# Feed-forward activations turned through memory in place of TensorE transposes, with the down products half a unit later

## The chip, the cores and the metric

One core of a Trainium2 chip runs the whole kernel. The metric is device time in microseconds (us) of one execution; lower is better. Engines are named as in the profile: PE (TensorE matmul), PEld (its weight load), DVE (VectorE), ACT (ScalarE), POOL (GpSimd), SP (SyncE, which here only issues DMAs).

## The reference

One layer on 256 tokens of width 2048 in float32: a mixer (an RWKV-7 half and a gated delta rule half), an output product, and a gated feed-forward block. Only the last part is touched here:

```python
x = x + y @ w_out[l]
h = rms_norm(x, ffn_norm_w[l])
x = x + (jax.nn.silu(h @ ffn_w_gate[l]) * (h @ ffn_w_up[l])) @ ffn_w_down[l]
return rms_norm(x, final_norm_w)
```

with `ffn_w_gate` and `ffn_w_up` of 2048 x 5632 and `ffn_w_down` of 5632 x 2048.

## The kernel before

Every float32 product is made of three products of halves: an operand is split into a high part (rounded to the matmul's own type, `wh`, by ACT, L202) and the rest (`wl`, by DVE, L203), and high x high, low x high and high x low are added up in PSUM. `load_split` (L177) fetches 512 KB of weights into one of three `raw` buffers with a DMA issued by SP (L184) and splits it in two halves of 512 columns into one of two pairs of `wh` and `wl`. All of this has high priority (`hi()`).

The feed-forward block takes the 44 blocks of 128 hidden columns in 11 units of four (`units`, c = 0, 4, ..., 40). For each unit:

- `gate(c1)` and `up(c1, sg)` call `gate_up` (L1049): 8 loads, and for each load 12 products (L1070) of 128 x 512 into two banks, one for each 128 tokens. The stationary operand is the activation x2 (hidden on partitions), the moving one the weights, so the result has tokens on partitions. ACT makes silu of the gate into `sg` (L1081), DVE multiplies the up result in (L1089).
- The down product needs the opposite: hidden columns on partitions, tokens in the free dimension. `turn(c1, sg)` (L1092) makes eight PE transposes of 128 x 128 (L1102) into PSUM banks `psT` and splits them into the tile `h` (high part in columns 0 to 255, rest in 256 to 511 of each of four blocks; L246 and L247).
- `down(c, h, hf)` (L1134), for half hf of the output columns: 4 loads, 12 products (L1147) for each, into four banks `psd` taken in turn from three tags, which DVE then adds to `acc` (L1155). `between` is called after the second load's products.

The order around the change is written out in the loop: gate of the next unit, first down of this unit, up of the next unit, second down of this unit with the next unit's turn in its middle. `beside` is a hook in `gate_up`, used in the first gate to turn x2 for the residual (`turn_x2`). The tiles of an engine are ordered by a list scheduler at build time, from priorities and a simulated timeline; `together` ties some instructions into a sequence on one engine. In unit 9 (c0 = 36) `gate_up` also fetches the down weights of the last unit (`raw_end`, L1062) one after another through one buffer and splits them into places handed out by `wend_slots` (`wend`), for the final products (L1196 to L1198).

The block way through memory that the change uses exists earlier in the kernel: `tri_inverse` stores a tile to DRAM in packets of 128 bytes (`sX`, L360), reads it back (`st`, L363) and turns 32 x 32 blocks on DVE (L369).

Of the kernel before, what the change touches and what calls it, by code (L numbers as in the profile page):

```python
# [49 lines left out]
def trunk_kernel(ctx, tc, xT, vecs, fnw, w_up, a_up, g_up, w_in, w_ab, w_out, w_gu, w_dn, out):  # L50
# [9 lines left out]
    def hi():  # L60
        return tc.high_priority(offset=HI)

    def together(ms, after=(), sync=True):

        kind = mybir.DependencyClass
        for a in after:
            tc.add_manual_dep(ms[0].ins, a.ins.name, mybir.DependencyInfo(kind.Sync, mybir.DependencyReason.DATA),
                              reason="together")
        for a, b in zip(ms, ms[1:]):
            tc.add_manual_dep(b.ins, a.ins.name, mybir.DependencyInfo(kind.NoSync, mybir.DependencyReason.DATA),  # L70
                              reason="together")

    def mps(name, tag="mr"):
        return pm.tile([P, 512], F32, tag=tag, name=name)
# [73 lines left out]
    class Side:  # L148
# [4 lines left out]
        def step(self):  # L153
            if self.cond is not None:
                if not self.cond():
                    return False
                self.cond = None
            try:
                self.cond = next(self.gen)
            except StopIteration:  # L160
                self.done = True
                side.remove(self)
            return True
# [8 lines left out]
            assert any([g.step() for g in list(side)])  # L172


    first = []

    def load_split(src, by_k=False, whole=False):  # L177

        with hi():
            if first:  # L180
                raw = first.pop(0)
            else:
                raw = wp.tile([P, 1024], F32, tag="raw", name="raw", bufs=RAW)
                SY.dma_start(out=raw.rearrange("p (c f) -> p c f", c=4) if by_k else raw, in_=src)  # L184
            wh = wp.tile([P, 1024], F32R, tag="wh", name="wh", bufs=WH)
            wl = wp.tile([P, 1024], F32R, tag="wl", name="wl", bufs=WL)
            both = [(wh[:, h * 512:h * 512 + 512], wl[:, h * 512:h * 512 + 512]) for h in range(2)]
            if whole:
                split(wh, wl, raw)
                return both  # L190
            it = iter(both)
            return halves_of(raw, lambda: next(it), by_k)
# [856 lines left out]
    def gate_up(c0, m, tag="pb", beside=None):  # L1049

        banks = [pm.tile([P, 512], F32, tag=tag, name="psq") for _ in range(2)]
        b = c0 + 2 * m - NFB + 8
        ends = [(x % 4, x // 4) for x in (b, b + 1, b + 4, b + 5)] if 0 <= b < 4 else []
        for q in range(2):
            for kk in range(4):
                if ends and kk % 2:
                    wend[ends[2 * q + kk // 2]] = halves_of(raw, own)
                elif ends:
                    raw = rp.tile([P, 1024], F32, tag="i1", name="raw_end")
                    i_, hf = ends[2 * q + kk // 2]  # L1060
                    with hi():
                        SY.dma_start(out=raw, in_=w_dn[NFB - 4 + i_, hf])  # L1062
                parts = load_split(w_gu[c0:c0 + 4, m, q, :, kk * 256:kk * 256 + 256].rearrange("c p f -> p c f"), True)
                for kx in range(2):
                    k = 8 * q + 2 * kk + kx
                    t, ri = x2k[k]
                    wh, wl = parts[kx]
                    for o, w in ((0, wh), (T, wh), (0, wl)):
                        for tb in range(2):
                            last = PE.matmul(banks[tb], t[:, ri, o + tb * P:o + tb * P + P], w,  # L1070
                                             start=(k == 0 and o == 0 and w is wh), stop=(k == KB - 1 and w is wl))
                if beside and kk % 2:
                    beside(2 * q + kk // 2, last)
        return banks

    def gate(c0, beside=None):
        banks = gate_up(c0, 0, beside=beside)
        sg = [fp.tile([P, 512], F32, tag="tg", name="sg", bufs=2) for _ in range(2)]
        with hi():
            for tb in range(2):  # L1080
                S.activation(sg[tb], banks[tb], AF.Silu, scale=rstd2[:, tb:tb + 1])  # L1081
        last_gate[0] = sg[1]
        return sg

    def up(c0, sg, tag="pb"):
        banks = gate_up(c0, 1, tag)
        with hi():
            for tb in range(2):
                V.scalar_tensor_tensor(sg[tb], banks[tb], rstd2[:, tb:tb + 1], sg[tb], ALU.mult, ALU.mult)  # L1089
        return sg  # L1090

    def turn(c0, sg, before=()):  # L1092

        h = act.tile([P, 4, 2 * T], F32R, tag="act", name=f"h{c0}")
        ps, ms = [], []
        for b in range(2):
            ps.append(mps("psT", ("mr", "mc", "mg")[nbank[0] % 3]))
            nbank[0] += 1
            for i in range(2):
                for tb in range(2):  # L1100
                    o = i * T + tb * P
                    ms.append(PE.transpose(ps[b][:, o:o + P], sg[tb][:, (2 * b + i) * P:(2 * b + i) * P + P], ident))  # L1102
        together([*before, *ms])
        for b in range(2):
            with hi():
                p3, hs = ps[b].rearrange("p (i t) -> p i t", i=2), slice(2 * b, 2 * b + 2)
                split(h[:, hs, 0:T], h[:, hs, T:], p3)
        return h

    nbank = [0]  # L1110

    def wend_slots():

        one = ["lw", "SB", "sq2", "bk", "i3"] + ["kt", "rt"] * 2 + ["vt"] * 4
        bufs = {"kt": 2, "rt": 2, "vt": 4}

        def places():
            x2w = rp.tile([P, 8, 512], F32R, tag="AT1", name="wend")
            for i in range(8):
                yield x2w[:, i, :]  # L1120
            w = act.tile([P, 4, 2 * T], F32R, tag="act", name="wend")
            for i in range(4):
                yield w[:, i, :]
            w = rp.tile([P, 2, 512], F32R, tag="Yt", name="wend")
            yield w[:, 0, :]
            yield w[:, 1, :]
            for t in one:
                yield rp.tile([P, 512], F32R, tag=t, name="wend", bufs=bufs.get(t, 1))
            for i in range(6):
                yield fp.tile([P, 512], F32R, tag=("wend", "sq2")[i // 4], name="wend", bufs=(4, 2)[i // 4])  # L1130
        g = places()
        return lambda: (next(g), next(g))

    def down(c0, h, hf, between=None):  # L1134
        n = 4
        banks = []
        for b in range(4):
            banks.append(mps("psd", ("mr", "mc", "mg")[nbank[0] % 3]))
            nbank[0] += 1
        for i in range(n):  # L1140
            parts = load_split(w_dn[c0 + i, hf])
            for tb in range(2):
                hh = h[:, i, tb * P:tb * P + P]
                hl = h[:, i, T + tb * P:T + tb * P + P]
                for st, w in ((hh, 0), (hh, 1), (hl, 0)):
                    for cg in range(2):
                        m = PE.matmul(banks[tb * 2 + cg], st, parts[cg][w],  # L1147
                                      start=(i == 0 and w == 0 and st is hh), stop=(i == n - 1 and st is hl))
            if between and i == 1:
                between(m)  # L1150
        for tb in range(2):
            for cg in range(2):
                cs = slice(hf * 1024 + cg * 512, hf * 1024 + cg * 512 + 512)
                with hi():
                    V.tensor_tensor(acc[:, tb, cs], acc[:, tb, cs], banks[tb * 2 + cg], ALU.add)  # L1155
# [3 lines left out]

    def turn_x2(i, before):  # L1160

        tb, ps = i // 2, [mps("ps_xn", t) for t in ("mr", "mc")]
        q0 = i % 2 * 2
        ms = [PE.transpose(ps[q][:, k * P:k * P + P], x2[:, 4 * (q0 + q) + k, tb * P:tb * P + P], ident)
              for q in range(2) for k in range(4)]
        together([before] + ms)
        for q in range(2):
            S.copy(acc[:, tb, (q0 + q) * 512:(q0 + q) * 512 + 512], ps[q])

    sg = gate(units[0], turn_x2)  # L1170
    h = turn(units[0], up(units[0], sg, "mg"))

    for c, c1 in zip(units, units[1:]):
        sg = gate(c1)
        down(c, h, 0)
        up(c1, sg)
        ahead = []
        down(c, h, 1, lambda m: ahead.append(turn(c1, sg, [m])))
        h = ahead[0]


    n = 4
# [110 lines left out]
```

## Time and profile before

| | |
|---|---|
| median of 3 runs | 1256.82 us (1255.65 to 1258.12) |
| profiled execution | 1255.44 us, of which the span of the profile is 1253.7 |
| granted PE clock | 0.995 |
| feed-forward block (first product of L1070 at 510.03 us) | about 740 us of the span |
| PE in the window of one unit, 591.65 to 657.84 | busy 66.19 of 66.19 us |
| DMA engines in the same window | 67% busy, 189 GB/s |

A row of the profile like `PE psT L1102` names the engine, the tile written and the line. In the chain of waits the first number is the start in us from the start of the span, the second the length, and `x8` the number of instructions. In rows of groups the two numbers behind the bar are busy time in us and the mean ns of one, and behind the next bar stands the idle time ahead of them and who ended it. Rows of waits give total us, times, and the longest. A row of a window gives the window, its length, each engine's busy time with its instructions (PE, PEld, DVE, ACT, POOL), and then the granted clock, the DMA engines' busy share and GB/s. DMA rows of a queue give packets, MB and the share of 16 engines' time.

### The profile page before, as it was taken

The page shows a single profiled execution, that of the slowest core. Times are in us where ns is not written, and L with a number is a line of the kernel's source. Part 1 is how long each engine was busy: PE and PEld are TensorE (multiplying, and loading weights), DVE is VectorE, ACT ScalarE, POOL GpSimd, SP SyncE. Part 2 cuts the span into 40 slices and gives each one's busy share as a digit, 9 for nine tenths or more (in the row PEclk, how much of TensorE's full clock was granted, in tenths as well). Part 3 has the DMA queues.
Part 4 walks back from the last instruction along what each step waited for, and adds up shares of the span by engine and source line. Part 5 has one row for each costly group of instructions (what it writes and reads, how often), then busy time and mean ns, then how long its engine had stood idle before and what let it go on. Part 6 is the DMA issues. An engine that isn't in the chain of part 4 may idle for free.

```text
span 1253.7 us, 21133 instructions
## 1 busy us (share of the span) xinstructions
PE 1234.8 (98%) x8134; PEld 1087.0 (87%) x8134; DVE 834.3 (67%) x1635; ACT 651.3 (52%) x1199; POOL 17.8 (1%) x63
## 2 busy tenths in 40 slices
PE   8999999999999999999999999999999999999997
PEld 8999999999999989888888888888888888878886
DVE  7987887977966877565555555555656565665554
ACT  7575665667546456554444444444444444454443
POOL 3000000000000000000000000000000000000000
PEclk9999999999999999999999999999999999999999
DMA  7455665575573445676666666666676666676641
GB/s 248 153 169 179 169 170 149 169 186 139 196 213 118 145 159 186 172 205 194 190 190 197 188 193 192 194 190 196 187 198 182 189 190 195 203 236 193 193 151 67
DMA packets 175702, 226.68 MB, mean 181 GB/s; under 512 B 52273, under 2 KB 144561, under 8 KB 175345
## 3 DMA queue, kind: packets, MB, share of 16 engines
q1 hardware_dynamic: 170896, 221.54, 60.4%
q10 hardware_dynamic: 4560, 2.74, 0.8%
q8 instruction: 64, 1.05, 0.4%
q0 software_dynamic: 144, 1.05, 0.2%
q14 instruction: 38, 0.30, 0.1%
HBM read 218.75 MB, written 4.46 MB: 178 GB/s over the span
## 4 chain that ended last, share of the span: by engine, by line
PE 88%; DVE 5%; DMA 3%; issue 1%; ACT 1%; SPq 0%; ACTq 0%; DVEq 0%
PE psq L1070 37%; PE psd L1147 17%; PE psb L220 16%; PE psb L223 8%; DVE wl L247 2%; PE psT L1102 1%; DMA sX_r<-X_r 1%; DMA raw_end<-in_w_dn 1%; DMA st_r<-sX_r 1%; PE ps_A L485 1%; PE psd L1198 1%; PE psd L1196 1%; PE psd L1197 1%; DMA A_g<-sG 0%; PE psSg L923 0%
## 5 line engine op out<-in xcount | busy, mean ns | idle before, releaser
L203 DVE TENSOR_TENSOR wl<-raw,wh 128x512 fp32r<-128x512 f32 x524 | 340.7, 692 | 273.5 <-ACT wh L202 271.8
L202 ACT ACTIVATE wh<-raw 128x512 fp32r<-128x512 f32 x524 | 302.5, 626 | 363.9 <-PE psq L1070 192.4
L1070 PE MATMUL psq<-wh,x2s 128*128 128x512 f32 x1408 | 377.4, 390 | 0.8 <-ACT wh L202 0.8
L1070 PEld LDWEIGHTS psq<-wh,x2s 128*128 128x128 f32 x1408 | 263.7, 188 | 56.2 <-ACT wh L202 1.7
L1070 PE MATMUL psq<-wl,x2s 128*128 128x512 f32 x704 | 217.2, 389 | 0.0
L220 PE MATMUL psb<-xs,wh 128*128 128x256 f32 x816 | 206.4, 287 | 2.4 <-ACT wh L202 1.7
L223 PE MATMUL psb<-xs,wh 128*128 128x256 f32 x816 | 206.0, 286 | 0.0
L1147 PE MATMUL psd<-wh,h 128*128 128x512 f32 x640 | 203.2, 391 | 1.0 <-ACT wh L202 1.0
L246 ACT ACTIVATE wh<-raw 128x1024 fp32r<-128x1024 f32 x128 | 135.4, 1058 | 87.4 <-PE psb L223 67.8
L247 DVE TENSOR_TENSOR wl<-raw,wh 128x1024 fp32r<-128x1024 f32 x128 | 156.1, 1220 | 11.1 <-ACT wh L246 10.9
L220 PEld LDWEIGHTS psb<-xs,wh 128*128 128x128 f32 x816 | 156.8, 192 | 4.4 <-ACT wh L202 2.4
L223 PEld LDWEIGHTS psb<-xs,wh 128*128 128x128 f32 x816 | 156.8, 192 | 1.2 <-issue 0.7
L1070 PEld LDWEIGHTS psq<-wl,x2s 128*128 128x128 f32 x704 | 132.0, 188 | 27.6
L1147 PEld LDWEIGHTS psd<-wh,h 128*128 128x128 f32 x640 | 119.2, 188 | 25.8 <-ACT wh L202 1.7
L220 PE MATMUL psb<-xs,wl 128*128 128x256 f32 x816 | 127.1, 287 | 0.9 <-DVE wl L247 0.7
L1147 PE MATMUL psd<-wl,h 128*128 128x512 f32 x320 | 124.6, 389 | 0.0
L220 PEld LDWEIGHTS psb<-xs,wl 128*128 128x128 f32 x816 | 109.8, 192 | 2.8 <-DVE wl L247 1.1
L1147 PEld LDWEIGHTS psd<-wl,h 128*128 128x128 f32 x320 | 60.1, 188 | 12.7
L223 PE MATMUL psb<-ys,wh 128*128 128x256 f32 x256 | 64.6, 288 | 2.5 <-DVE ys L247 2.5
L220 PE MATMUL psb<-ys,wh 128*128 128x256 f32 x256 | 64.8, 289 | 0.2 <-ACT ys L246 0.2
L223 PEld LDWEIGHTS psb<-ys,wh 128*128 128x128 f32 x256 | 50.1, 196 | 2.8 <-DVE ys L247 2.7
L1155 DVE TENSOR_TENSOR acc<-acc,psd 128x512 f32<-128x512 f32 x80 | 49.5, 682 | 1.8 <-PE psd L1147 1.8
(315 smaller groups left out, 1026.8 us busy)
## 6 DMA issues: line engine op xcount, KB each, us to landing
raw<-in_w_gu SPq DMA_DIRECT2D x176, 512.0 KB, 4.9
raw<-in_w_in SPq DMA_DIRECT2D x99, 512.0 KB, 3.5
raw<-in_w_dn SPq DMA_DIRECT2D x80, 512.0 KB, 4.3
raw<-in_w_out SPq DMA_DIRECT2D x32, 512.0 KB, 3.5
raw_end<-in_w_dn SPq DMA_DIRECT2D x8, 512.0 KB, 4.2
xraw<-in_xT SPq DMA_DIRECT2D x8, 256.0 KB, 5.8
x<-in_xT SPq DMA_DIRECT2D x1, 2048.0 KB, 9.7
raw<-in_w_ab SPq DMA_DIRECT2D x2, 512.0 KB, 4.9
```

The costliest lines, as they stand in the source:

```text
L202: S.activation(oh, src, AF.Copy)
L203: V.tensor_tensor(ol, src, oh, ALU.subtract)
L220: PE.matmul(ps[:, 0:T], w, rt[:, ri, 0:T], start=(first and k == 0 and not low), stop=(last and k == 7 and low == 1))
L223: PE.matmul(ps[:, 0:T], w, rt[:, ri, T:], start=False, stop=False)
L246: S.activation(hi_ap, src, AF.Copy)
L247: V.tensor_tensor(lo_ap, src, hi_ap, ALU.subtract)
L485: PE.matmul(psA[h][:, ch, :], bk[hr, ch].rearrange("p a t -> p (a t)"), ar[hr, p, ch].rearrange("p a t -> p (a t)"), start=True, stop=True)
L1070: last = PE.matmul(banks[tb], t[:, ri, o + tb * P:o + tb * P + P], w, start=(k == 0 and o == 0 and w is wh), stop=(k == KB - 1 and w is wl))
L1102: ms.append(PE.transpose(ps[b][:, o:o + P], sg[tb][:, (2 * b + i) * P:(2 * b + i) * P + P], ident))
L1147: m = PE.matmul(banks[tb * 2 + cg], st, parts[cg][w], start=(i == 0 and w == 0 and st is hh), stop=(i == n - 1 and st is hl))
L1155: V.tensor_tensor(acc[:, tb, cs], acc[:, tb, cs], banks[tb * 2 + cg], ALU.add)
L1196: PE.matmul(ps, hh, wh, start=(i == 0), stop=False)
```

## The change

Units 0 to 9 are no longer turned by PE. `turn_far(c0, sg)` makes two VectorE block transposes (`V.transpose`, 32 x 32 blocks, on 128 x 512 each) into tiles `tn0` and `tn1` (tags i2 and i3), which puts the tokens of each block of 32 into the free dimension but leaves the blocks where they were. Eight DMAs of 64 KB store `tn` in a DRAM tile `sH` in runs of 128 bytes, and four DMAs of 128 KB read it back, in runs of 1 KB, into the second half of the tile `h`, with the hidden columns on partitions. One split over all four blocks then makes the high and the low part. All twelve DMAs are issued by SP, each group tied behind the last weight load (`loads[-1]`). They are placed by the hook `step`, which is now called after every load's products in both gate and up of the next unit: stores at steps 2 to 5 (in the gate), reads at steps 8 to 11 and the split at step 14 (in the up).

The downs of a unit come half a unit later to give this the time: gate of the next unit, second down of the unit before last (`late`), up of the next unit, first down of this unit. The last unit is turned by PE as before, in the last second down. The i3 slot is taken from the places of the last unit's weights.

```diff
-                SY.dma_start(out=raw.rearrange("p (c f) -> p c f", c=4) if by_k else raw, in_=src)
+                loads.append(SY.dma_start(out=raw.rearrange("p (c f) -> p c f", c=4) if by_k else raw, in_=src))
...
-                if beside and kk % 2:
-                    beside(2 * q + kk // 2, last)
+                if beside:
+                    beside(4 * q + kk, last)
...
-    def up(c0, sg, tag="pb"):
-        banks = gate_up(c0, 1, tag)
+    def up(c0, sg, tag="pb", beside=None):
+        banks = gate_up(c0, 1, tag, beside)
...
+    def turn_far(c0, sg):
+
+        tn = []
+        for tb in range(2):
+            tn.append(rp.tile([P, 512], F32, tag=("i2", "i3")[tb], name=f"tn{tb}"))
+            with hi():
+                V.transpose(tn[tb], sg[tb])
+        h = act.tile([P, 4, 2 * T], F32R, tag="act", name=f"h{c0}")
+        raw = h[:, :, T:].bitcast(F32)
+
+        sH = dr.tile([32, 16, 8, 32], F32, name=f"sH{c0}")
+        rows = sH.rearrange("r (i q) b c -> q r i (b c)", q=4)
+
+        def step(n, last):
+            with hi():
+                if 2 <= n < 6:
+                    tb, a0 = n // 2 - 1, n % 2 * 2
+                    ds = [SY.dma_start(out=sH[:, :, 4 * tb + a, :],
+                                       in_=tn[tb][32 * a:32 * a + 32].rearrange("r (j c) -> r j c", c=32))
+                          for a in (a0, a0 + 1)]
+                elif 8 <= n < 12:
+                    ds = [SY.dma_start(out=raw[32 * q:32 * q + 32], in_=rows[q]) for q in (n - 8,)]
+                else:
+                    ds = []
+                if ds:
+                    together([loads[-1]] + ds)
+                if n == 14:
+                    split(h[:, :, 0:T], h[:, :, T:], raw)
+        return h, step
...
-        one = ["lw", "SB", "sq2", "bk", "i3"] + ["kt", "rt"] * 2 + ["vt"] * 4
+        one = ["lw", "SB", "sq2", "bk"] + ["kt", "rt"] * 2 + ["vt"] * 4
...
     def turn_x2(i, before):
 
+        if i % 2 == 0:
+            return
+        i //= 2
...
     sg = gate(units[0], turn_x2)
-    h = turn(units[0], up(units[0], sg, "mg"))
-
+    h, step = turn_far(units[0], up(units[0], sg, "mg"))
+
+    late = None
     for c, c1 in zip(units, units[1:]):
-        sg = gate(c1)
+        sg = gate(c1, step)
+        if late:
+            down(*late, 1)
+        up(c1, sg, "pb" if late else "mg", lambda n, last: step(8 + n, last))
         down(c, h, 0)
-        up(c1, sg)
-        ahead = []
-        down(c, h, 1, lambda m: ahead.append(turn(c1, sg, [m])))
-        h = ahead[0]
+        late = c, h
+        if c1 != units[-1]:
+            h, step = turn_far(c1, sg)
+    ahead = []
+    down(*late, 1, lambda m: ahead.append(turn(units[-1], sg, [m])))
+    h = ahead[0]
```

More of the change, by code (lines that the diff above doesn't have):

```diff
@@ L172, in drain @@
             assert any([g.step() for g in list(side)])
-    first = []
+    first, loads = [], []
     def load_split(src, by_k=False, whole=False):
```

## The prediction

> **What bounds the kernel.** I read the page first, then the chain of waits in one feed-forward unit, then who waits for whom on PE, ACT and SP, then the DMA queue in short windows.
>
> ```profile
> span 1253.7 us, 21133 instructions
> PE 1234.8 (98%) x8134; PEld 1087.0 (87%) x8134; DVE 834.3 (67%) x1635; ACT 651.3 (52%) x1199; POOL 17.8 (1%) x63
> ...
> L246 ACT ACTIVATE wh<-raw 128x1024 fp32r<-128x1024 f32 x128 | 135.4, 1058 | 87.4 <-PE psb L223 67.8
> L247 DVE TENSOR_TENSOR wl<-raw,wh 128x1024 fp32r<-128x1024 f32 x128 | 156.1, 1220 | 11.1 <-ACT wh L246 10.9
> ```
> ```profile
> 591.65 21.76 PE psq L1070 x96
> 613.41 5.44 PE psd L1147 x24
> 618.86 0.87 PE psT L1102 x8
> 619.73 5.47 PE psd L1147 x24
> 625.20 21.76 PE psq L1070 x96
> 646.96 10.88 PE psd L1147 x48
> 657.84 21.76 PE psq L1070 x96
> ```
>
> The second fence is the chain of waits over one unit (start, length, what): an up, the second down with the turn in its middle, a gate, the first down, the next up. The chain never leaves PE. From 591.65 to 657.84 a unit lasts 66.19 us and holds 288 products: 21.76/96 = 0.2267 us each, 65.28 in all. The rest, 66.19 - 65.28 = 0.91 us, is the turn (0.87) and the products beside it (5.47 against 5.44).
>
> ```profile
> PE psd L1147 <- ACT wh L202: 1.0, 1, 1.0
> PE psq L1070 <- ACT wh L202: 0.8, 2, 0.5
> ```
> ```profile
> ACT wh L202 <- PE psq L1070: 192.4, 128, 2.1
> ACT wh L202 <- PE psd L1147: 111.0, 74, 2.0
> ACT wh L202 <- DMA raw<-in_w_gu: 32.5, 18, 2.8
> ...
> ACT wend L202 <- DMA raw_end<-in_w_dn: 12.6, 6, 3.3
> ```
>
> These are PE's waits and ACT's waits in this stage (us in total, times, longest). PE waits 1.8 us in it. ACT, which makes the high halves of the weights, mostly waits for PE to give back a buffer (303 us), much less for a weight load (32.5). So PE is the bound, and what leaves PE's queue leaves the time, as long as weights come no later than this:
>
> ```profile
> 671.02 1.16 ACT L202 ACTIVATE wh<-raw 128x512 fp32r<-128x512 f32 x2 [1.56 <-PE psq L1070]
> ...
> 671.88 1.29 DVE L203 TENSOR_TENSOR wl<-raw,wh 128x512 fp32r<-128x512 f32 x2 [1.62 <-ACT wh L202]
> ...
> 674.00 1.07 PE L1070 MATMUL psq<-wh,x2s 128*128 128x512 f32 x4
> ...
> 674.90 0.61 PE L1070 MATMUL psq<-wl,x2s 128*128 128x512 f32 x2
> ...
> 679.41 1.41 DVE L1089 SCALAR_TENSOR_TENSOR sg<-psq,rstd,sg 128x512 f32<-128x512 f32 x2 [0.99 <-PE psq L1070]
> ...
> 690.58 2.48 DVE L1155 TENSOR_TENSOR acc<-acc,psd 128x512 f32<-128x512 f32 x4
> ```
>
> In this timeline the block that PE starts at 674.00 is split at 671.02 (ACT, first half done by 671.60) and 671.88 (DVE, first half done by 672.53, needed at 674.90). A split may thus start 2.4 us late before PE stands. The idle time in brackets (1.56 on ACT) is in every 2.72 us step.
>
> **The change, part by part.**
>
> *Taken off PE.* Units 0 to 9 lose their eight transposes; unit 10 keeps them. 10 x 0.91 = 9.1 us, all on the path. The other products are the same, in another order; the turning of x2 (turn_x2) happens at the same four places, since every second call of eight now returns at once. Between gate and up lies now the second down of the unit before; the accumulators alternate as before, so I cost the reordering at nothing. What covers it is the evacuation beside the next products (2.48 us of DVE above, with PE not waiting). Only at the end do two downs follow each other, and the second needs two of the first's banks 6 products (1.36 us) in: 0 to 1 us, once; I take 0.3.
>
> *Added on DVE and ACT.*
>
> ```profile
> L369 DVE STREAM_TRANSPOSE tn_r<-st_r x2: 446/446/446, 185.8 to 271.1; 128x256 f32<-128x256 f32 x2
> ...
> L246 ACT ACTIVATE h<-psT x22: 579/584/599, 562.2 to 1219.0; 128x512 fp32r<-128x512 f32 x22
> L247 DVE TENSOR_TENSOR h<-psT,h x22: 682/684/692, 562.8 to 1219.9; 128x512 fp32r<-128x512 f32 x22
> ```
> ```profile
> 591.65:657.84 66.19, 66.19 (x298) 54.89 (x297) 38.17 (x61) 29.88 (x52) 0.00 (x0) 1.00 0.67 189
> ```
>
> Two block transposes of 512 columns, 2 x 2 x 0.446 = 1.8 us a unit on DVE. The splits of h change from two of 0.584 and 0.684 to one of 1.06 (ACT) and 1.22 (DVE). By the windows row DVE is busy 38.17 of 66.19 us and would be 39.8 of 65.3. A transpose of 0.9 or a split of 1.2 fits an idle gap of some 1.4, and the 2.48 of L1155 passes without a wait of PE. Cost taken: nothing; bounds 0 to 0.3 us a unit.
>
> *Added on SP and the DMA engines.* Per unit eight stores of 64 KB (512 packets of 128 bytes each), two behind each of four gate loads, and four loads of 128 KB (128 packets of 1 KB each) behind four up loads.
>
> ```profile
> DMA packets 1811, 0.26 MB, mean 171 GB/s; under 512 B 1804, under 2 KB 1804, under 8 KB 1811
> ...
> q1 hardware_dynamic: 1811, 0.26, 103.3%
> ```
> ```profile
> DMA packets 9480, 12.50 MB, mean 189 GB/s; under 512 B 381, under 2 KB 8453, under 8 KB 9477
> ...
> q1 hardware_dynamic: 9477, 12.46, 67.2%
> ```
> ```profile
> L360 SPq DMA_DIRECT2D sX_r<-X_r x4: 551/660/827, 177.8 to 261.3; - x4
> ```
> ```profile
> SPq L184 <- DVE wl L203: 504.5, 228, 3.7
> ```
>
> The first fence is the window 180.0 to 181.5, when the triangular inverse stores 128-byte packets in DRAM: 1811 packets with all engines busy, so 1.5 x 16 / 1811 = 13.3 ns a packet, 0.85 us for the 1024 of one step. The second is the unit above: 24 weight loads take 67.2% of 66.19 us, 1.85 us each. A step with stores needs 1.85 + 0.85 = 2.70 of its 2.72 us: the queue is full for four steps but falls behind by nothing. A read step adds 128 packets at no more than the unit's mean of 44.5 x 16 / 9477 = 75 ns, 0.6 us, which fits. On SP two stores are issued in 2 x 0.66 = 1.3 us, inside the 504.5/228 = 2.2 us that it waits before each load for DVE to free a raw buffer; behind them stand only later loads. Cost taken: nothing.
>
> The DMA page of the Trainium skill (DMA: Bandwidth & Descriptors, Specifications) speaks against this: below 512 bytes the DMA does a read-modify-write. If that doubled my 13.3 ns the gain would be gone (worked out under the rivals), but those 13.3 ns are themselves stores of 128 bytes to DRAM, so the row already holds it, and the row decides.
>
> *New waits.* The stores wait on SP for the transposes. SP runs ahead:
>
> ```profile
> 670.29 8.49 SPq L184 DMA_DIRECT2D raw<-in_w_dn  x4
> ...
> 679.44 1.07 PE L1147 MATMUL psd<-wh,h 128*128 128x512 f32 x4
> ```
>
> a load is issued 9.2 us before its products, so the third gate load goes out 3.7 us before the gate, 7.2 after the end of the up (a down of 10.88 lies between). The transposes are done 1.4 + 1.8 = 3.2 us after the up. Unit 0 has no down there: if SP's order holds the first store at that place, SP stands some 6 us and PE at most 6 - 2.4 = 3.6, once. I take 0.3, since the order of an engine's queue is laid out ahead of time with work that can run put first: in the chain's rows on unit 0
>
> ```profile
> 536.27 25.46 PE psq L1070 x112
> 561.74 0.87 PE psT L1102 x8
> ```
> ```profile
> raw<-in_w_gu SPq DMA_DIRECT2D x176, 512.0 KB, 4.9
> ...
> sX_r<-X_r SPq DMA_DIRECT2D x4, 128.0 KB, 4.6
> ```
>
> the up's 96 products are followed by 16 of the next gate, and only then by the turn, which the program has first. The reads come at least three loads (8 us) behind the stores, against 4.6 us from issue to landing of the sX_r stores on the page. The split of h then stands in ACT's order, ahead of the next weight split, until the last read has landed. Its cover is ACT's 1.56 us gap and the 2.4 above: a wait w costs PE w + 1.06 - 1.56 - 2.4 us, nothing up to 2.9. The nearest row is ACT's wait for raw_end, 12.6/6 = 2.1 us, longest 3.3. I take 0; bounds 0 to 0.4 a unit.
>
> ```profile
> 1088.50:1112.73 24.23, 22.39 (x97) 17.46 (x96) 15.23 (x25) 12.83 (x24) 0.00 (x0) 1.00 0.81 261
> ```
>
> *The last weights.* In the gate of unit 9, raw_end loads come on top and the gate lasts 24.23 us instead of 21.76: 2.5 us already lost to waits like these. Here the stores come on top again, and the i3 slot is gone from the list of places: bounds from -2.5 (the loads move to another place and the loss goes) to +4 x 0.85 = +3.4; I take +0.5.
>
> **Sum.** The profiled execution took 1255.44 us (span 1253.7). 1255.44 - 9.1 + 0.3 + 0.3 + 0.5 = 1247.4. The median of the runs shown is 1256.82, 1.4 above the profiled one, so 1248.8 is my time, 0.64% faster.
>
> **Rivals.**
>
> *The h split eats part of it.* ACT waits for the read in its order longer than the cover. At 3.3 us, the longest raw_end wait, it costs 0.4 us a unit: 1253. With the bounds of DVE (0.3) and unit 9 too, 1255. For: DMA landings that ACT's order didn't foresee stand in the rows. Against: six such waits in a gate at 81% DMA cost 2.5 us together.
>
> *Slower: the same wait at full length.* From w = 3.8 us on, the loss (0.91 a unit) outweighs the turn. If ACT stood a whole landing of a gate load (4.9 us on the page), 4.9 + 1.06 - 1.56 - 2.4 = 2.0 a unit, 1256.8 + 10 x (2.0 - 0.9) = 1268. The rows' 3.3 stays short of the point.
>
> *Slower or even: dear packets.* Stores at a stride of 1 KB, beside weights, might cost more than those of the inverse. With p ns a packet four steps fall behind by 4 x (1.85 + 0.064 p - 2.72); less the 2.4 of cover this reaches 0.91 at p = 26.5, twice the row: then no change. At 40 ns it is 6.8 - 2.4 - 0.9 = 3.4 a unit, 1290.
>
> *It does nothing:* the weights can't come 1.4% faster, and the time goes from the turn to waits for wh, 1255 to 1257. Against it: ACT waits for PE, not for loads, in 303 us, and DMA has a third of its time left.
>
> **Chances.** My forecast 0.62 (own range 1245.5 to 1251.5); the h split eating part 0.16 (three quarters of it still below 1254.3); nothing 0.08; the long wait 0.08; dear packets 0.06, a third of it at no change. About 0.2% (2.5 us) is what a measurement here tells from no change. Faster: 0.62 + 0.12 = 0.74. Same: 0.04 + 0.08 + 0.02 = 0.14. Slower: 0.12. The range 1245.5 to 1257.5 leaves out the slower cases and a few percent below.
>
> **What the profile after would show.** Right: psT with 8 transposes instead of 88; units of 65.3 us in the chain; two STREAM_TRANSPOSE of about 0.89 us a unit; DMA share of a unit near 0.75; ACT's wait for h below 2.9 us; PE's waits in this stage still a few us. Wrong: PE waiting for wh or wl once in each unit, near the gate's third to sixth load (packets) or behind the split of h (long wait). The store step is wrong if its windows show the DMA engines full and gate loads landing 3 us later than 4.9.

## The result, and the profile after

The changed kernel takes 1266.26 us in the median of 8 runs (1259.45 to 1270.2), the one before 1257.14 of 8 (1255.25 to 1259.74): 0.7% slower, ratio 1.0068 with a 95% interval of 1.0043 to 1.0092. The forecast was 1248.8, and 1257.5 at most.

The page of the changed kernel (span, engines, chain, landing of DMAs):

```profile
span 1266.7 us, 21161 instructions
...
PE 1234.3 (97%) x8054; PEld 1077.5 (85%) x8054; DVE 844.7 (67%) x1645; ACT 649.0 (51%) x1189; POOL 17.8 (1%) x63
...
PE 73%; DMA 12%; DVE 9%; ACT 3%; issue 2%; SPq 1%; ACTq 0%; DVEq 0%
...
raw<-in_w_gu SPq DMA_DIRECT2D x176, 512.0 KB, 5.6
...
sH<-tn SPq DMA_DIRECT2D x80, 64.0 KB, 5.2
h<-sH SPq DMA_DIRECT2D x40, 128.0 KB, 6.2
```

The 80 transposes are gone, and yet PE is busy as long as before (1234.8) in a span 13 us longer. The chain now holds 12% of DMA and 9% of DVE (3 and 5 before). Gate and up weights land 5.6 us after issue, not 4.9. Who waited for whom from 505 us on, PE first, then ACT:

```profile
PE psq L1070 <- ACT wh L202: 11.1, 10, 4.6
```
```profile
ACT wh L202 <- DMA raw<-in_w_gu: 126.7, 63, 4.6
...
ACT wh L202 <- PE psq L1070: 90.9, 71, 3.2
ACT h L246 <- DMA h<-sH: 25.0, 10, 4.8
```

ACT stands 25.0 us for the reads of h, once for each of the ten units turned in this way, and 126.7 us for gate and up loads, which was 32.5. The chain through one unit shows how a wait for h leads to a long wait for a load (most of the 126.7 us stay when no wait for h is left, and cost nothing, as late_split shows below):

```profile
712.83 8.17 PE psd L1177 x36
721.03 0.64 ACT wh L202
721.69 1.30 DVE wl L203 x2
723.01 0.37 SPq L184
723.38 0.05 issue
723.43 6.62 DMA h<-sH
730.07 1.07 ACT h L246
731.16 0.07 DVE h L247
...
732.31 1.30 DVE wl L203 x2
733.62 6.77 DMA raw<-in_w_gu
...
740.50 0.64 ACT wh L202
...
741.18 5.78 PE psq L1070 x24
746.96 10.88 PE psd L1177 x48
```

The last read is issued at 723.43 and lands 6.6 us later. Only then does ACT split h, and behind it in ACT's and DVE's order stand the next weight splits. So a raw buffer comes free late (733.62), the load that it was wanted for lands at 740.4, and now PE stands. From 712.83 to 746.96 a down and an up took 34.13 us for 144 x 0.2267 = 32.64: 1.49 lost, more than the 0.91 of a turn. ACT's timeline in the same stretch has both waits, each in the brackets:

```profile
726.89 1.15 ACT L202 ACTIVATE wh<-raw 128x512 fp32r<-128x512 f32 x2 [1.99 <-DMA raw<-in_w_gu]
730.07 1.06 ACT L246 ACTIVATE h<-h 128x1024 fp32r<-128x1024 f32 x1 [2.03 <-DMA h<-sH]
731.04 2.18 ACT L202 ACTIVATE wh<-raw 128x512 fp32r<-128x512 f32 x4
734.73 1.15 ACT L202 ACTIVATE wh<-raw 128x512 fp32r<-128x512 f32 x2 [1.52 <-PE psq L1070]
740.50 1.15 ACT L202 ACTIVATE wh<-raw 128x512 fp32r<-128x512 f32 x2 [4.61 <-DMA raw<-in_w_gu]
```

ACT waits 2.03 us for h, catches up, and 5 us later waits 4.61 for a weight load.

The dearest place is unit 0 to 1, where no down lies between up, gate and up (timeline of PE, then windows):

```profile
579.36 1.21 PE L1070 MATMUL psq<-wh,x2s 128*128 128x512 f32 x4 [1.66 <-ACT wh L202]
...
595.15 2.08 PE L1070 MATMUL psq<-wh,x2s 128*128 128x512 f32 x4 [4.57 <-ACT wh L202]
```
```profile
579.36:590.00 10.64, 10.64 (x47) 8.78 (x48) 5.16 (x8) 5.08 (x9) 0.00 (x0) 1.00 0.82 190
595.15:605.00 9.85, 9.85 (x31) 7.86 (x32) 5.41 (x9) 3.81 (x7) 0.00 (x0) 0.69 0.54 133
605.00:614.61 9.61, 9.61 (x44) 7.97 (x43) 4.34 (x8) 3.88 (x7) 0.00 (x0) 1.00 0.64 195
```

PE stands (has no work) 1.66 and 4.57 us, and in the 9.85 us after the long stand its granted clock is 0.69.

The losses by place, here and in the runs below, worked out from the starts of the groups of products in each trace, less 0.2267 us a product and 0.11 a transpose. The first gate's own 4.5 us (the sum of squares and turn_x2) are taken off. The raw_end loads belong to unit 9, but the order laid out at build time may place them earlier (in most of these kernels two of the eight stand beside unit 0): in the kernel before the loss is at the gate of unit 9, in the changed kernel and several others at the gate or up of unit 8. The column takes units 8 and 9 together.

| kernel | unit 0 to 1 | raw_end (units 8 and 9) | other units |
|---|---|---|---|
| before | 0 | 2.9 | 0 |
| changed | 10.5 | 5.3 | 6.6 |
| no_way | 0 | 4.4 | 0 |
| stores_only | 1.8 | 5.8 | 0 |
| reads_only | 10.3 | 4.5 | 4.5 |
| late_split | 2.9 | 4.9 | 0 |
| order_only | 0.6 | 2.8 | 0 |
| late_unit0 | 0 | 6.6 | 0 |
| late_ends | 1.3 | 1.1 | 0 |
| late_ends_5 (the same kernel) | 2.5 | 4.0 | 0 |
| late_unit0_ends | 0 | 2.1 | 0 |
| late_unit0_ends_2 (the same kernel) | 0 | 0.3 | 0 |
| before_ends | 0 | 0 | 0 |

Each row is one profiled execution. The two rows of late_ends differ by 1.2 and 2.9 us, so a difference of that size between single rows is no measured cost; and the row of no_way is from an execution of 1249.3 us, 3.4 below its median.

The changed kernel loses 22.4 us where the one before loses 2.9, and saves 9.1: 10.4 slower in this stage. The two profiled executions differ by 13.0 us, the medians by 9.1. The other 2.5 us between the two spans lie before the stage, in code that both share: the first product of L1070 starts between 509.9 and 513.1 us in the twelve different kernels profiled here (509.9 in the one before, 512.3 in the changed one, 512.7 in before_ends, which turns as before).

### The profile page after: what moved, and what is told of

Read it like the earlier page. It is cut to its first block, busy times and chain, and to the rows that moved or that the text cites. A ratio compares the mean times of both kernels' runs of the same rounds, so it can differ in the third digit from the quotient of the medians.

```text
span 1266.7 us, 21161 instructions
## 1 busy us (share of the span) xinstructions
PE 1234.3 (97%) x8054; PEld 1077.5 (85%) x8054; DVE 844.7 (67%) x1645; ACT 649.0 (51%) x1189; POOL 17.8 (1%) x63
## 4 chain that ended last, share of the span: by engine, by line
PE 73%; DMA 12%; DVE 9%; ACT 3%; issue 2%; SPq 1%; ACTq 0%; DVEq 0%
PE psq L1070 29%; PE psd L1177 15%; PE psb L220 14%; PE psb L223 7%; DMA h<-sH 3%; DMA raw<-in_w_gu 2%; DVE wl L247 2%; DMA raw_end<-in_w_dn 2%; DVE wl L203 1%; DMA raw<-in_w_in 1%; ACT wh L202 1%; DMA sX_r<-X_r 1%; PE ps_A L485 1%; DVE wend L203 1%; PE psd L1237 1%
## 5 line engine op out<-in xcount | busy, mean ns | idle before, releaser
L202 ACT ACTIVATE wh<-raw 128x512 fp32r<-128x512 f32 x524 | 301.1, 623 | 350.0 <-DMA raw<-in_w_gu 126.7
L1070 PE MATMUL psq<-wh,x2s 128*128 128x512 f32 x1408 | 381.4, 393 | 11.3 <-ACT wh L202 11.1
L1070 PEld LDWEIGHTS psq<-wh,x2s 128*128 128x128 f32 x1408 | 264.2, 189 | 71.5 <-ACT wh L202 16.8
L1070 PE MATMUL psq<-wl,x2s 128*128 128x512 f32 x704 | 219.2, 392 | 1.3 <-DVE wl L203 0.7
L1177 PE MATMUL psd<-wh,h 128*128 128x512 f32 x640 | 200.6, 390 | 0.0
L247 DVE TENSOR_TENSOR wl<-raw,wh 128x1024 fp32r<-128x1024 f32 x128 | 156.1, 1220 | 10.3 <-ACT wh L246 10.0
L1070 PEld LDWEIGHTS psq<-wl,x2s 128*128 128x128 f32 x704 | 131.8, 189 | 32.7 <-DVE wl L203 5.2
```

Of the source, the lines that this page charges most:

```text
L202: S.activation(oh, src, AF.Copy)
L247: V.tensor_tensor(lo_ap, src, hi_ap, ALU.subtract)
L1177: m = PE.matmul(banks[tb * 2 + cg], st, parts[cg][w], start=(i == 0 and w == 0 and st is hh), stop=(i == n - 1 and st is hl))
```

## The experiments

Theory 1: ACT's split of h stands in its order until late reads land, and what it holds up comes back as late weight loads. Theory 2: the 128-byte stores fill the DMA queue. Theory 3: the new order, or DVE, costs the time.

**no_way** drops both branches with DMAs in `step` and splits from the block transposes:

```diff
-                    split(h[:, :, 0:T], h[:, :, T:], raw)
+                    for tb in range(2):
+                        o = tb * P
+                        split(h[:, :, o:o + P], h[:, :, T + o:T + o + P], tn[tb].rearrange("p (i t) -> p i t", i=4))
```

> Leaves out all twelve DMAs of each unit; h is split straight from the block transposes (so it holds the wrong tokens and hidden columns), at the same step. Theory 1 (ACT's split of h stands in its order until the reads land, and what it holds up comes back as late weight loads) and theory 2 (the 128-byte stores fill the DMA queue and make the gate loads late) both expect the removed transposes to show: 1248 to 1251 us against 1257 before. Theory 3 (the new order of downs or the DVE transposes cost the time themselves): 1257 or more.

1252.69 us (1247.63 to 1254.08), ratio to before 0.9947 (0.9924 to 0.9969). The median is 1.7 us above the range expected, but theory 3 is out: in the table this kernel loses nothing outside the raw_end column. The saving of the transposes is real; the way through memory takes it.

**stores_only** has the same split and keeps the stores.

> Leaves out the reads; the stores stay, h is split straight from the block transposes (wrong values). Theory 1: nearly all of the loss is gone, 1248 to 1253 us. Theory 2: 1258 us or more, with PE waiting for weights in the gates.

1252.75 us (1251.95 to 1254.01), ratio 0.9962 (0.9947 to 0.9977). The median is that of no_way (1252.69), which has no stores. In the single profiles the eighty stores of 128-byte packets lose 1.8 us in unit 0, 1.4 more at raw_end, which is inside the spread of that column, and nothing in the other units. Theory 2 falls as the main cause.

**reads_only** makes the stores in unit 0 alone:

```diff
+    same = []
...
-        sH = dr.tile([32, 16, 8, 32], F32, name=f"sH{c0}")
+        if c0 == 0:
+            same.append(dr.tile([32, 16, 8, 32], F32, name="sH"))
+        sH = same[0]
...
-                if 2 <= n < 6:
+                if c0 == 0 and 2 <= n < 6:
```

> Leaves out the stores of all units but unit 0; every unit reads unit 0's tile (wrong values). Unit 0 keeps both stores and reads and so its 10.6 us. Theory 1: 1262 to 1266 us, ACT's wait for h stays at 20 to 25 us in all. Theory 2: 1254 to 1259 us, and the gate loads land in 4.9 us again.

1266.27 us (1263.16 to 1269.31), ratio 1.0069 (1.0048 to 1.009): as slow as the changed kernel, as theory 1 had it (0.3 above its range). Gate and up loads land after 5.2 us on its page. ACT's waits in it (from 510 to 1230 us):

```profile
ACT wh L202 <- DMA raw<-in_w_gu: 89.9, 39, 4.5
ACT h L246 <- DMA h<-sH: 22.9, 10, 4.3
```

The wait for h is nearly whole (22.9 of 25.0), with no stores behind unit 0. The other units lose 4.5 us in its profile against 6.6 with stores; whether stores add to the reads there, one profile of each doesn't tell.

**late_split** leaves all twelve DMAs and their places, and ties only ACT's part of the split behind a later weight split:

```diff
-            S.activation(oh, src, AF.Copy)
+            highs.append(S.activation(oh, src, AF.Copy))
...
                 if n == 14:
-                    split(h[:, :, 0:T], h[:, :, T:], raw)
+                    high = S.activation(h[:, :, 0:T], raw, AF.Copy)
+                    V.tensor_tensor(h[:, :, T:], raw, h[:, :, 0:T], ALU.subtract)
+                    together([highs[-1], high])
```

> Computes the whole; ACT's part of the h split is tied behind the weight split of the seventh up load (step 14), some 7 us after the last read lands. Theory 1: the waits of ACT for h go (from 25 us to under 2) and with them 6 to 9 us: 1257 to 1260 us, the loss of unit 0 to 1 stays. Theory 2: no change, 1264 to 1268 us.

1254.58 us (1253.3 to 1256.04), ratio to before 0.9977 (0.9966 to 0.9989): 12 us faster than the changed kernel by the medians, more than expected, since 7.6 of unit 0's 10.5 go as well. The loss of the other units is zero. In the answer on the tile h (changed kernel, then late_split), under "its engine sat idle before it":

```profile
  DMA h<-sH: 25.0, 10
```
```profile
  ACT h L1137: 1.6, 9
```

Nothing waits for a read any more (1.6 us is DVE waiting for ACT), and the reads land as late as before, 6.1 us in the median: the place of the split in ACT's order cost the time, not the amount of data. ACT's waits for gate and up loads (510 to 1230 us) are hardly fewer than the 126.7 us of the changed kernel:

```profile
ACT wh L202 <- DMA raw<-in_w_gu: 108.9, 64, 4.1
```

The loss is gone all the same, outside the first two columns of the table. So these waits as such don't cost PE anything; what cost it, by the chain above, were those that a held-up split made too long for the buffers to cover. A unit in its chain is bare products, 65.28 us:

```profile
705.36 10.88 PE psd L1179 x48
716.24 21.76 PE psq L1070 x96
738.00 10.88 PE psd L1179 x48
748.88 21.76 PE psq L1070 x96
```

**order_only** turns every unit by PE, in the new order:

```diff
-        up(c1, sg, "pb" if late else "mg", lambda n, last: step(8 + n, last))
-        down(c, h, 0)
+        up(c1, sg, "pb" if late else "mg")
+        ahead = []
+        down(c, h, 0, (lambda m: ahead.append(turn(c1, sg, [m]))) if c1 != units[-1] else None)
```

> Computes the whole; the downs in the new order, but every unit turned by PE in the middle of its predecessor's first down; no block transposes, no way through memory. If the new order itself costs nothing (theory 1): within 2 us of before, 1255 to 1259 us. If the order costs: 1260 us or more.

1258.5 us (1256.16 to 1260.83), ratio 1.0008 (0.9996 to 1.0019). The order costs nothing that shows: 1.0 us by this ratio, with an interval from -0.5 to 2.4.

**early_reads** issues the reads at steps 6 to 9 in place of 8 to 11.

> Computes the whole; the changed kernel with the four reads two steps earlier (behind gate loads 7 and 8 and up loads 1 and 2 in place of up loads 1 to 4); the split is not tied. Theory 1a (ACT's place for the split follows the landing that the build-time order assumes, wherever the reads stand): the split moves ahead with them, ACT still waits 2 us or so a unit, 1262 to 1268 us. Theory 1b (the reads are merely too late for a fixed place): the waits go, 1254 to 1257 us.

1314.2 us (1309.7 to 1316.51), ratio 1.0444 (1.0415 to 1.0473). Both expectations missed by 50 us. SP's waits from 580 to 1260 us, and ACT's for h from 505 us on:

```profile
SPq L1131 <- DMA sH<-tn: 21.5, 19, 3.4
```
```profile
ACT h L246 <- DMA h<-sH: 42.4, 9, 5.8
```

Now the first reads follow the last stores by one step and must wait on SP until these have landed (5.2 us on its page). SP stands up to 3.4 us, and the weight loads behind it stand too. The split moved ahead with the reads, as theory 1a has it, but with two changes at once this run doesn't tell 1a from 1b. It shows that one step between the last store and the first read is too little for SP's queue; distances between that and the changed kernel's weren't run.

**late_unit0** is late_split with

```diff
-    h, step = turn_far(units[0], up(units[0], sg, "mg"))
+    h, step = turn(units[0], up(units[0], sg, "mg")), lambda n, last: None
```

> Computes the whole; the tied split of the run late_split, and unit 0 turned by PE as before. Unit 0 has no down between its up and the next gate, so its stores stand close behind the transposes; late_split still loses 2.9 us there. If the way through memory causes that: 1252 to 1254 us (2.9 gained, 0.9 paid for the turn). If it is the raw_end loads beside it: 1255 us, no gain.

1252.31 us (1250.96 to 1252.83), ratio 0.9958 (0.9941 to 0.9975). Unit 0's loss is gone, as expected if the way through memory made it.

**late_ends** is late_split with raw_end loads spread and their splits tied:

```diff
-        b = c0 + 2 * m - NFB + 8
-        ends = [(x % 4, x // 4) for x in (b, b + 1, b + 4, b + 5)] if 0 <= b < 4 else []
+        g = (c0 - NFB + 12) // 2 + m
+        ends = [(x % 4, x // 4) for x in (0, 1, 4, 5, 2, 3, 6, 7)[2 * g:2 * g + 2]] if 0 <= g < 4 else []
...
+                if ends and kk == 2:
+                    behind, n0 = highs[-1], len(highs)
+                    wend[ends[q]] = halves_of(raw, own)
+                    together([behind, *highs[n0:]])
```

> Computes the whole; the tied split, and the eight raw_end loads spread over the gates and ups of units 8 and 9, one for each four weight loads, their ACT splits tied two loads later. Late_split loses 4.9 us in unit 9 and 2.9 in unit 0, where ACT stands for raw_end loads. If the same cause (a split placed ahead of its landing in ACT's order) makes these: 1248 to 1252 us. If the DMA engines are simply full there: 1254 us or more.

1250.61 us (1246.65 to 1252.94), ratio 0.9938 (0.9915 to 0.9961), inside the range of the first cause. This edit spreads the loads as well as tying the splits, so it doesn't say which of the two did more.

**late_ends_5**, the same kernel again:

> The same kernel as late_ends, in more rounds, to have its ratio beside the next run's: 1248 to 1252 us.

1250.61 us (1248.03 to 1251.67), ratio 0.9945 (0.9932 to 0.9959).

**late_unit0_ends** joins the last two.

> Computes the whole; late_ends with unit 0 turned by PE. late_ends still loses 1.3 us in unit 0; the turn costs 0.9. If that loss is the way through memory: 0.4 us faster than late_ends, inside the noise; if the raw_end loads had been its cause it is 0.9 slower.

1247.86 us (1247.34 to 1249.69), ratio 0.9929 (0.9918 to 0.994). Faster than late_ends by 2.7 us, more than the 0.4 expected; in the profile of late_ends_5 unit 0 lost 2.5 us rather than 1.3, so that loss varies from run to run. PE's waits in this stage (510 to 1230 us):

```profile
PE psq L1072 <- ACT wh L202: 1.7, 1, 1.7
```

**before_ends** puts only the raw_end part into the kernel before, and **late_unit0_ends_2** runs the best kernel beside it.

> Computes the whole; the kernel before (all units turned by PE, its own order) with only the raw_end loads spread and tied as in late_ends. If the 2.9 us that before loses in unit 9 come from ACT standing for raw_end loads: 1253 to 1255 us, and the rest of the gain of late_unit0_ends (about 6 us) is the way through memory. If it reaches 1249 or less, the way through memory is worth nothing.

> The same kernel as late_unit0_ends, beside before_ends on one chip: 1247 to 1250 us.

before_ends: 1253.92 us (1251.77 to 1256.42), ratio 0.997 (0.9955 to 0.9985). late_unit0_ends_2: 1246.98 us (1244.9 to 1248.54), ratio 0.9913 (0.9894 to 0.9931). The profile of before_ends loses nothing at raw_end, where the kernel before loses 2.9. So the raw_end part is worth 3.3 us by itself, and turning nine units through memory 6.9 more, of 9 x 0.91 = 8.2 that it takes off PE. This kernel beats the one before by 0.9% and the changed one by 19 us.

## Why the prediction was wrong

*What held.* Taken off PE: 0.91 us a unit; a unit of late_split lasts the 65.28 us worked out. The new order at nothing: order_only. DVE's work at nothing: no_way. The packets: the DMA share of a unit is 0.78 (0.75 forecast), and the rival of dear packets fell with stores_only. The block transposes took even less than their 0.89 us:

```profile
562.67 0.71 DVE L1116 STREAM_TRANSPOSE tn<-sg 128x512 f32<-128x512 f32 x1
```

*The step that failed: the split of h, its cover counted as ACT's gap plus 2.4 us, "nothing up to 2.9".* ACT waited 25.0/10 = 2.5 us a unit. In the units after the first only two of the nine waits were longer than 2.9 us:

```profile
863.12 1.06 ACT L246 ACTIVATE h<-h 128x1024 fp32r<-128x1024 f32 x1 [3.39 <-DMA h<-sH]
...
1131.51 1.06 ACT L246 ACTIVATE h<-h 128x1024 fp32r<-128x1024 f32 x1 [3.28 <-DMA h<-sH]
```

By the formula of the prediction these would have cost 0.5 + 0.4 = 0.9 us in all and the others nothing. PE lost 6.6 us in these units, 1.49 of them behind a wait of 2.03. The 2.4 us was read off as the time by which one split may be late. But a late split also gives its raw buffer back late, and a load needs 5.6 us (6.8 at 733.62 above) of the 3 x 2.72 = 8.2 us that three buffers last, with 2.0 for the split: some 0.6 us is left by this estimate, where I had put 2.9. The wait is passed on to a later load, and PE stands there, not behind the split of h. That the split's place made the loss is shown by late_split; the passing on round the buffers is read from the chain of one unit, and the 0.6 us itself wasn't measured. I had the landing time (4.9) and the number of buffers and didn't go round that loop. The mechanism was named as a rival at 0.16 and, for the slower side, at 0.08; both were priced with the same cover, which gives nothing for the 2.5 us that ACT waited. That the second one's 1268 us lies near the measured 1266 is luck: it takes 4.9 us of wait in every unit, where 2.5 was measured, and has nothing for unit 0. The first one's 1255 isn't the sum of its own terms either: 1248.8 + 10 x (0.4 + 0.3) + 2.9 = 1258.7, above the top of the range.

*Undersized: the landing of the reads.* I weighed the wait by raw_end (2.1 us on average, 3.3 longest). The reads of a quarter as many bytes land after 6.2 us in the median, longer than the 4.9 of a whole gate load before. Why 128 KB takes that long isn't settled: they follow a 512 KB load in the same queue, and each writes 32 partitions; neither was taken apart.

*Undersized: unit 0, costed at 0.3 with a bound of 3.6; it was 10.5.* I looked only at SP standing for the transposes. That was small, since SP's order did put loads first. What the runs show is the wait for h with no down in between: late_split takes 7.6 of the 10.5 away, PE turning unit 0 the rest. Of the 10.5 us 6.2 are PE's stands and about 3.1 the low clock behind the second (72 products in 19.46 us, 16.32 at the usual rate); 1.2 are not assigned.

```profile
595.15 19.46 PE psq L1070 x72
```

*The last weights, +0.5 with a bound of +3.4:* +2.4, inside the bounds, but the reason given isn't shown. I had put it down to the stores; no_way, which has none, already loses 4.4 there, 1.5 more than the kernel before, and two profiles of one kernel differ by more than the 2.4.

The Trainium skill has a rule on stores below 512 bytes (DMA: Bandwidth & Descriptors, Specifications: a read-modify-write), which I set aside for the row. It did no harm here: stores_only loses nothing in the units between the first and raw_end.

## What to carry to other kernels

When a transfer is hidden behind other work, ask in which engine's order its consumer stands: an instruction that is placed by an assumed landing holds up everything behind it when the landing is late, and tying it behind work that is later than the landing costs a few lines and gave 12 us here. Count the cover of a wait round the whole buffer loop (issue, landing, consumer, release), not from the first consumer's slack, because a stall is handed on to the load that reuses the buffer. Saving PE time paid here only where the loads that feed it kept some of that loop free.

## What was not expected of the hardware

A long stand of PE can cost more than its own length. After 4.57 us without work the granted clock read 0.69 over the next 9.85 us (windows above), and the 72 products behind it took 19.46 us in place of 16.32; after the stand of 1.66 us it stayed at 1.00. The Trainium skill (TensorE: Matmul & The Clock Gate, HAM oscillation — how this bites in real kernels) says that an idle gap above about 3.4 us makes the clock gate throttle the array again. The two stands here lie on either side of that, but early_reads doesn't fit it: there the clock fell after a stand of 2.59 us, to 0.64 over the next 4.80 (timeline of PE, then the window). The measurement decides: a stand need not reach 3.4 us.

```profile
731.82 1.64 PE L1070 MATMUL psq<-wh,x2s 128*128 128x512 f32 x4 [2.59 <-ACT wh L202]
```
```profile
731.82:736.62 4.80, 4.50 (x12) 3.14 (x13) 4.80 (x8) 1.78 (x4) 0.00 (x0) 0.64 0.06 14
```

In late_split it stayed at 1.00 after one of 2.15 us:

```profile
1056.90 1.20 PE L1070 MATMUL psq<-wh,x2s 128*128 128x512 f32 x4 [2.15 <-ACT wh L202]
```
```profile
1056.90:1061.70 4.80, 4.80 (x21) 3.92 (x22) 3.25 (x6) 2.81 (x6) 0.00 (x0) 1.00 0.65 195
```

Where the limit lies, and whether the length of the stand alone sets it, these runs don't settle.
